# TensorE kept in the order of the program's text, in a kernel of two transformer blocks

## The chip, the core and the metric

The kernel runs on one core of a Trainium2 chip. The core has five engines that run side by side: TensorE (PE in the profile; PEld is its load of weights), VectorE (DVE), ScalarE (ACT), GpSimd (POOL) and SyncE (SP, which here only issues transfers). Each engine takes its instructions strictly from a queue of its own, and semaphores make one engine wait for another. The metric is the device time of one execution, in microseconds, as the median of several runs.

## What is computed

The input is 512 tokens of 1024 features in fp32. Two blocks follow each other. Cut to what matters:

```python
def first_block(x, ...):
    p = split(rms_norm(x, norm_g) @ w_in)                 # q, k, v, o, z, gates, attention parts
    mq, mk = silu(conv4(p.m_q)), silu(conv4(p.m_k))       # causal convolutions over 4 tokens
    mh = mlstm(mq, mk, p.m_v, p.m_i + b_i, p.m_f + b_f)   # 4 heads of 256, running maximum of the gates
    ya = sigmoid(p.m_o) * head_layernorm(mh) * silu(p.m_z)
    kc, vc = gelu(blocks(k) @ w1) @ w2, ...               # compressed keys and values
    yb = sparse_attention(q, kc, vc, ...) * silu(p.n_z)
    x = x + (sigmoid(p.g_a) * (ya @ w_a) + sigmoid(p.g_b) * (yb @ w_b)) @ w_out
    return rms_norm(x, final_g)

def second_block(x, c, ...):
    shift, scale, gate = silu(c) @ ada_w + ada_b
    x = x + 0.5 * gate[0] * swiglu(modulate(rms_norm(x)), ffn1)
    x = x + gate[1] * token_mixer(modulate(rms_norm(x)))  # pooling branch and gated delta rule
    x = x + 0.5 * gate[2] * swiglu(modulate(rms_norm(x)), ffn2)
    return rms_norm(x, final_g)

def gated_delta_rule(q, k, v, g, beta):                   # 8 heads of 128
    a = strict_lower(beta * (k @ k.T) * decay)
    u, w = solve(1 + a, beta * v), solve(1 + a, beta * exp(gc) * k)
    for chunk in chunks:                                  # S: state of 128 x 128
        v_new = u - w @ S
        o = (q * exp(gc)) @ S + (q @ k.T * decay) @ v_new
        S = S * exp(g_last) + k_dec.T @ v_new
```

## The kernel before

Values and weights are split into a high and a low part, both of a type that TensorE multiplies quickly, and each product of fp32 values is three matmuls into the same bank of PSUM: high with high, low with high, high with low. In the rows the parts end in h and l (`hh` and `hl` of the normed h, `uh` and `ul` of the values before the norm's factor, `wh` and `wl` of the weights). ACT rounds a piece of weights or values to the high part, DVE (sometimes POOL) subtracts for the low part. The result of a large product, whatever it is, is called `pg`.

A plan (`block1`, `ffn`, `mixer`) lists the large products group by group; `run` goes through it, piece of weights by piece. After each piece it calls `side_step`, which lets some generators go on by a step each: the side work, that is norms, the mLSTM, the attention, and in the mixer the delta rule. So the text of the program is already an interleaving: 12 matmuls of a large product (four 128-row tiles, three parts each), a few small matmuls of side work, 12 matmuls again.

What the steps of the prediction touch:

- Norms: `sq_add` sums squares on DVE or POOL (`nacc`), ones turn them into column sums (`nsum`), and a broadcast (`rb`) gives every row the factors.
- Gates of the first block (`mlstm_gates`): logarithms of the forget gates (`lf`) go through triangles and ones into a bank `gcol`; a scan on DVE (line 1255) gives the running maximum `mrow`, and four more matmuls put it into the same bank. Score products of the mLSTM are `mS`, from `mqk`, which DVE makes behind the convolutions (`ca`, `ct`).
- Compression: first layer `cps`, second layer `vcp`.
- Delta rule. `delta` prepares a head: transposes `dkt`, `dqt`, `dvt`, decays `dD`, products `dgq`, from which DVE makes `dB` and `ddm`; `dB` goes to memory (`bdr`). `delta_solve` inverts the triangles of 32 tokens of two heads (GS = 2) on DVE: it reads them from memory (`sd`), and 31 columns follow, each a multiply (`svt`) and a subtract (`su`), four columns a step; the result goes to memory twice (`udr`, `tdr`). SOLVE_DELAY = 7 steps later `delta_out` reads it back (`dum`, `dtm`, and `dbm` of `dB`), doubles the blocks on TensorE (`diq`, `diu`, twice), runs the recurrence over four chunks (`dks`, `dy`, `dso` on TensorE, `dws`, `dot` on DVE), applies norm and gate (`dot<-dot,db,zs`), and transposes (`doT`). There are four solves, 0 to 3, for heads 0 and 1, 2 and 3, and so on.

What sets the order: the tile framework has a list scheduler, which puts the instructions of each engine in an order of its own, by its own estimates of when operands are ready. A context, `in_order`, exempts the engines that are named in it:

```python
    def in_order(self, which):
        e = {"P": mybir.EngineType.PE, "A": mybir.EngineType.Activation, "D": mybir.EngineType.DVE,
             "G": mybir.EngineType.Pool}
        return self.tc.manual_schedule(engines={e[w] for w in which})
```

In the kernel before it stands at one place, for ACT and DVE at the beginning of the first block (`block1`, line 732); a few single instructions are kept in their place besides (lines 468, 683). TensorE is scheduled everywhere. By the trace, 540 of 9629 matmuls run later than matmuls that come after them in the text; the last of them ends at about 1494 us.

Of the kernel before, what the change touches and what calls it, by code (L numbers as in the profile page):

```python
# [18 lines left out]
P = 128  # L19
T = 512  # L20
D = 1024
# [7 lines left out]
GS = 2                  # heads whose triangles are solved together  # L29
SOLVE_STEP = 4          # columns of them between two products  # L30
SOLVE_DELAY = 7         # steps until the solved ones are back from memory
NV = 2                  # groups of values, of gates, that start before a norm
# [63 lines left out]
def prep(a):  # L96
    """Lays the inputs out for the loads: name -> array."""
# [4 lines left out]
    w = a["w_in"][0]  # L102
    o = {}
    at = 0
# [53 lines left out]
class Group:  # L158
    """One group of a large product: pieces of weights, and what to do with them."""
# [9 lines left out]
class Call:  # L169
    """A place in the plan where something else is put into the program."""  # L170
# [6 lines left out]
class Builder:  # L177
# [56 lines left out]
    def trr(self, out, in_):  # L234
        """transpose of values that float32r holds"""
        return self.nc.tensor.transpose(out.bitcast(F32R), in_, self.identr)
# [9 lines left out]
    def pow(self, out, in_, n):  # L246
        """out = in ** -0.5"""
        self.nc.gpsimd.tensor_tensor(out, in_, self.mhalf[:, 0:n], OP.pow)
# [34 lines left out]
    def later(self, f, *a):  # L283
        """evacuate now, or when the norm that the values lack is there"""
# [11 lines left out]
    def load(self, upto):  # L296
        """starts the loads of the weights, up to a piece"""
# [8 lines left out]
    def part(self, upto):  # L306
        """splits weights into the two parts that the products take"""
# [15 lines left out]
    def run(self, plan, ahead_dma=3, ahead_split=2):  # L323
# [5 lines left out]
        for g in plan:  # L329
# [6 lines left out]
            for k0, n in g.pieces:  # L336
# [4 lines left out]
                if g.early:  # L341
                    # whole tiles of tokens, one after another: the first in banks of the side work
# [35 lines left out]
                elif g.halves:  # L378
                    if k0 == 0:
                        ps = [self.pg.tile([P, 512], F32, tag="g", name="pg") for _ in range(2)]  # L380
                    if g.mid and k0 + n == g.kts:
                        # the first half of the tokens is done before the second
# [66 lines left out]
    def copies(self):  # L449
        """of the constants, in other types"""  # L450
# [11 lines left out]
    def rows_to_bcast(self, cols4, name, inorder=False):  # L462
        """[128, 4] token columns -> a bank [128, 512] with every row the 512 values"""
# [7 lines left out]
    def colsum(self, sq, ps, c0):  # L471
        """sums over features of sq, as token columns ps[:, c0 + t]"""
# [15 lines left out]
    def rstd(self, ps, c0, name):  # L488
        """token columns: (sum / D + eps) ** -0.5"""
# [6 lines left out]
    def u_add(self, f, x, g, shift=None):  # L496
        """x * g, split, for the products that start before the norm is known; the shift beside it"""
# [8 lines left out]
    def unorm(self, pa, pb):  # L506
        """the product with the norm, and the column that the shift adds"""
# [1455 lines left out]
```

## Time and profile before

| | us |
|---|---|
| three runs | 2001.44, 1997.78, 1995.58 |
| median | 1997.78 |
| span of the profiled execution | 1991.7 |
| TensorE busy in it | 1922.1 |
| VectorE busy | 1142.3 |
| ScalarE busy | 872.8 |
| GpSimd busy | 509.6 |

The profiled execution is one of its own; its span goes from its first to its last instruction. The stages in it: first block to about 707 us, first feed-forward part to 1081, mixer with the delta rule to about 1640, second feed-forward part and final norm to the end.

How to read the rows further down: a group of the timeline gives the start, the duration, the engine, the source line (often that of a helper), the operation, out and inputs, sizes, and in brackets the time that the engine stood idle just ahead, with what ended it. Matmuls overlap: one of 512 columns lasts 0.40 us, and the next starts 0.23 us after it. The granted clock (PEclk) is a share of 2.4 GHz; 0.50 is 1.2 GHz.

### The profile page before, as it was taken

The page shows a single profiled execution, that of the slowest core. Times are in us where ns is not written, and L with a number is a line of the kernel's source. Part 1 is how long each engine was busy: PE and PEld are TensorE (multiplying, and loading weights), DVE is VectorE, ACT ScalarE, POOL GpSimd, SP SyncE. Part 2 cuts the span into 40 slices and gives each one's busy share as a digit, 9 for nine tenths or more (in the row PEclk, how much of TensorE's full clock was granted, in tenths as well). Part 3 has the DMA queues.
Part 4 walks back from the last instruction along what each step waited for, and adds up shares of the span by engine and source line. Part 5 has one row for each costly group of instructions (what it writes and reads, how often), then busy time and mean ns, then how long its engine had stood idle before and what let it go on. Part 6 is the DMA issues. An engine that isn't in the chain of part 4 may idle for free. (4 is left out here: it accounts for less than half of the span.)

```text
span 1991.7 us, 27380 instructions
## 1 busy us (share of the span) xinstructions
PE 1922.1 (97%) x10296; PEld 1586.3 (80%) x10296; DVE 1142.3 (57%) x2059; ACT 872.8 (44%) x1856; POOL 509.6 (26%) x376
## 2 busy tenths in 40 slices
PE   8999999998999999999999999999999999999998
PEld 7779878786677888888888888867778897888887
DVE  7777674746655775333333769768755565333322
ACT  6565654656544443222222555645443343222221
POOL 2454443356621270000001433132210060000000
PEclk9999998999999999999999999999999999999999
DMA  5444445454311423333333233232332333333322
GB/s 182 137 147 143 159 136 174 148 187 160 109 43 37 154 78 102 94 93 92 103 109 109 80 94 88 85 100 67 82 105 85 122 101 96 95 95 95 95 88 72
DMA packets 100118, 216.21 MB, mean 109 GB/s; under 512 B 24721, under 2 KB 35857, under 8 KB 99985
## 3 DMA queue, kind: packets, MB, share of 16 engines
q1 hardware_dynamic: 95232, 208.27, 33.1%
q10 hardware_dynamic: 4752, 6.18, 1.0%
q8 instruction: 81, 1.33, 0.3%
q14 instruction: 53, 0.43, 0.1%
HBM read 206.55 MB, written 7.34 MB: 107 GB/s over the span
## 5 line engine op out<-in xcount | busy, mean ns | idle before, releaser
L217 ACT ACTIVATE wh<-wr 128x1024 fp32r<-128x1024 f32 (+4 forms) x311 | 315.2, 1014 | 643.3 <-issue 366.4
L220 DVE TENSOR_TENSOR wl<-wr,wh 128x1024 fp32r<-128x1024 f32 (+4 forms) x289 | 357.2, 1236 | 390.4 <-ACT wh L217 383.0
L229 PE MATMUL pg<-hh,wh 128*128 128x512 f32 x1240 | 501.2, 404 | 1.3 <-DVE un L220 1.3
L229 PE MATMUL pg<-hl,wh 128*128 128x512 f32 x1240 | 493.0, 398 | 0.9 <-DVE hl L226 0.9
L229 PE MATMUL pg<-hh,wl 128*128 128x512 f32 x1240 | 492.4, 397 | 0.0
L229 PEld LDWEIGHTS pg<-hh,wl 128*128 128x128 f32 x1240 | 234.5, 189 | 54.7 <-issue 0.2
L229 PEld LDWEIGHTS pg<-hh,wh 128*128 128x128 f32 x1240 | 235.4, 190 | 52.4 <-issue 2.1
L229 PEld LDWEIGHTS pg<-hl,wh 128*128 128x128 f32 x1240 | 235.1, 190 | 52.1 <-DVE hl L226 1.4
L220 POOL TENSOR_TENSOR adaw<-adaw,sc 128x512 f32<-128x512 f32 x144 | 216.4, 1523 | 228.5 <-DMA adaw<-in_ada 199.1
L220 POOL TENSOR_TENSOR nacc<-nacc,sq 128x512 f32<-128x512 f32 x34 | 47.6, 1406 | 786.4 <-ACT sq L217 786.3
L229 PE MATMUL pg<-wh,hh 128*128 128x256 f32 (+2 forms) x512 | 161.1, 315 | 11.2 <-ACT ca L217 8.8
L229 PE MATMUL pg<-wh,hl 128*128 128x256 f32 (+2 forms) x512 | 153.2, 302 | 1.0 <-DVE hl L220 0.7
L229 PE MATMUL pg<-wl,hh 128*128 128x256 f32 (+2 forms) x512 | 153.9, 301 | 0.0
L229 PE MATMUL pg<-fah,wh 128*128 128x512 f32 (+1 forms) x374 | 140.1, 382 | 0.0
L229 PE MATMUL pg<-fah,wl 128*128 128x512 f32 (+1 forms) x374 | 139.9, 381 | 0.0
L229 PE MATMUL pg<-fal,wh 128*128 128x512 f32 (+1 forms) x374 | 139.7, 380 | 0.0
L217 ACT ACTIVATE adaw<-adaw 128x512 f32<-128x512 f32 x144 | 90.9, 632 | 111.2 <-POOL adaw L220 109.1
L226 DVE SCALAR_TENSOR_TENSOR ca<-cx,cols,ca 128x511 f32<-128x511 f32 (+2 forms) x120 | 113.8, 948 | 24.3 <-ACT ca L217 22.3
L229 PEld LDWEIGHTS pg<-wh,hh 128*128 128x128 f32 x512 | 98.8, 193 | 21.2 <-ACT ca L217 9.7
L229 PEld LDWEIGHTS pg<-wl,hh 128*128 128x128 f32 x512 | 98.5, 192 | 4.6 <-issue 1.2
L229 PEld LDWEIGHTS pg<-wh,hl 128*128 128x128 f32 x512 | 97.9, 192 | 5.2 <-DVE hl L220 2.1
L220 POOL TENSOR_TENSOR wl<-wr,wh 128x1024 fp32r<-128x1024 f32 (+2 forms) x22 | 48.5, 2206 | 178.3 <-ACT wh L217 160.1
(431 smaller groups left out, 3217.8 us busy)
## 6 DMA issues: line engine op xcount, KB each, us to landing
adaw<-in_ada SPq DMA_DIRECT2D x144, 256.0 KB
wr<-in_f1i SPq DMA_DIRECT2D x44, 512.0 KB
wr<-in_f2i SPq DMA_DIRECT2D x44, 512.0 KB
wr<-in_m_qkv SPq DMA_DIRECT2D x24, 512.0 KB
wr<-in_w_o SPq DMA_DIRECT2D x16, 512.0 KB
wr<-in_f1o SPq DMA_DIRECT2D x16, 512.0 KB
wr<-in_m_g SPq DMA_DIRECT2D x16, 512.0 KB
wr<-in_f2o SPq DMA_DIRECT2D x16, 512.0 KB
```

Of the source, the lines that this page charges most:

```text
L217: return self.nc.scalar.activation(out, in_, f, bias=bias, scale=scale, **k)
L220: return (eng or self.nc.vector).tensor_tensor(out, a, b, op)
L226: return self.nc.vector.scalar_tensor_tensor(out, a, s, b, op0=op0, op1=op1, **k)
L229: return self.nc.tensor.matmul(out, lhsT, rhs, start=start, stop=stop, **k)
```

## The change

`kernel` wraps the whole build in the context, for TensorE alone. DVE, ACT, POOL and SP stay with the scheduler, which orders them anew around the fixed order. Besides, comments and docstrings are gone all over the file; they are left out here.

```diff
@@ -1956,7 +1956,9 @@
     with tile.TileContext(nc) as tc:
         with ExitStack() as ctx:
-            Builder(ctx, tc, A, out, coff).build()
+            b = Builder(ctx, tc, A, out, coff)
+            with b.in_order("P"):
+                b.build()
     r = run_bass_kernel_spmd(nc, [dram], core_ids=[0])
```

What that does to the order shows at three places. (Numbers behind names tell buffers apart; all of those of the changed kernel are higher by two.) First, TensorE at the gates of the first block, before: the columns of `lf`, then products; the columns of `mrow` stand at row 272, behind 27 products.

```order
242 L229 MATMUL pg_663<-hh_454,wl_383 128x512
243 L229 MATMUL gcol_676<-lf_583,cst_91 128x16 x2
244 L229 MATMUL gcol_676<-lf_583,ones_119 128x16
245 L229 MATMUL pg_663<-hh_491,wh_382 128x512
246 L229 MATMUL pg_663<-hl_492,wh_382 128x512
247 L229 MATMUL pg_663<-hh_491,wl_383 128x512
248 L229 MATMUL pg_663<-hh_524,wh_382 128x512
```

The same place on TensorE in the changed kernel:

```order
242 L229 MATMUL pg_665<-hh_456,wl_385 128x512
243 L229 MATMUL gcol_678<-lf_585,cst_93 128x16 x2
244 L229 MATMUL gcol_678<-lf_585,ones_121 128x16
245 L229 MATMUL gcol_678<-cst_93,mrow_652 128x4 x4
246 L229 MATMUL pg_665<-hh_493,wh_384 128x512
247 L229 MATMUL pg_665<-hl_494,wh_384 128x512
248 L229 MATMUL pg_665<-hh_493,wl_385 128x512
```

The columns of `mrow` moved ahead of the 27 products. Second, TensorE at the block inverse of heads 0 and 1 (`diq`), before: the matmuls are strewn among products of a later group, `pg_11664`.

```order
5955 L229 MATMUL pg_11664<-hl_10060,wh_11422 128x512
5956 L229 MATMUL pg_11664<-hh_10059,wl_11423 128x512
5957 L229 MATMUL diq_11516<-dtm_11444,dbm_11445 32x32
5958 L229 MATMUL pg_11664<-hh_10067,wh_11422 128x512
5959 L229 MATMUL pg_11664<-hl_10068,wh_11422 128x512
5960 L229 MATMUL pg_11664<-hh_10067,wl_11423 128x512
5961 L229 MATMUL pg_11664<-hh_10075,wh_11422 128x512
5962 L229 MATMUL pg_11664<-hl_10076,wh_11422 128x512
5963 L229 MATMUL diq_11516<-dtm_11444,dbm_11445 32x32 x7
5964 L229 MATMUL pg_11664<-hh_10075,wl_11423 128x512
```

TensorE at the same matmuls in the changed kernel:

```order
5919 L229 MATMUL pg_11430<-hl_10090,wh_11283 128x512
5920 L229 MATMUL pg_11430<-hh_10089,wl_11284 128x512
5921 L229 MATMUL diq_11518<-dtm_11446,dbm_11447 32x32 x8
5922 L229 MATMUL diq_11530<-dtm_11462,dbm_11463 32x32 x8
5923 L229 MATMUL pg_11556<-hh_9972,wh_11352 128x512
5924 L229 MATMUL pg_11556<-hl_9973,wh_11352 128x512
```

All sixteen moved ahead, in front of the group `pg_11556` (`pg_11554` before) and of `pg_11664`. Third, VectorE at the gates of heads 0 and 1 (`dot<-dot,db,zs`), which TensorE's `doT` waits for, before: columns of solve 1 (`svt`, `su`) stand among them.

```order
1303 L220 TENSOR_TENSOR svt<-sd,su 32x207
1304 L220 TENSOR_TENSOR da<-drq 128x4
1305 L226 SCALAR_TENSOR_TENSOR dot<-dot,db,zs 128x128
1306 L220 TENSOR_TENSOR su<-su,svt 32x23x9
1307 L220 TENSOR_TENSOR da<-da,doss 128x4
1308 L226 SCALAR_TENSOR_TENSOR dot<-dot,db,zs 128x128
1309 L220 TENSOR_TENSOR svt<-sd,su 32x192
1310 L223 TENSOR_SCALAR da<-da 128x4
1311 L226 SCALAR_TENSOR_TENSOR dot<-dot,db,zs 128x128
1312 L220 TENSOR_TENSOR su<-su,svt 32x24x8
1313 L226 SCALAR_TENSOR_TENSOR dot<-dot,db,zs 128x128
1314 L220 TENSOR_TENSOR svt<-sd,su 32x175
```

VectorE at the same gates in the changed kernel:

```order
1315 L226 SCALAR_TENSOR_TENSOR ca<-cx,cols,ca 128x510
1316 L223 TENSOR_SCALAR da<-da 128x4
1317 L226 SCALAR_TENSOR_TENSOR ca<-cx,cols,ca 128x509
1318 L223 TENSOR_SCALAR drq<-drn 128x4
1319 L226 SCALAR_TENSOR_TENSOR db<-db,drq 128x4
1320 L220 TENSOR_TENSOR da<-drq 128x4
1321 L226 SCALAR_TENSOR_TENSOR dot<-dot,db,zs 128x128
1322 L220 TENSOR_TENSOR da<-da,doss 128x4
1323 L226 SCALAR_TENSOR_TENSOR dot<-dot,db,zs 128x128
1324 L226 SCALAR_TENSOR_TENSOR dqkv<-ct,ca 128x512
1325 L223 TENSOR_SCALAR da<-da 128x4
1326 L226 SCALAR_TENSOR_TENSOR dot<-dot,db,zs 128x128 x2
```

The solve moved ahead: its last column stands at row 1307 now, in front of all the gates; before it stood at row 1338, behind them.

## Rows read from the trace of the kernel before

**Rows 1.** The page's first part: busy time, share of the span, instructions of each engine.

```profile
PE 1922.1 (97%) x10296; PEld 1586.3 (80%) x10296; DVE 1142.3 (57%) x2059; ACT 872.8 (44%) x1856; POOL 509.6 (26%) x376
```

**Rows 2.** Table by stage: window, length, then each engine's busy time; last, PEclk, DMA share, GB/s.

```profile
core 0 of [0], span 1991.7 us
...
0.00:90.00 90.00, 76.74 (x465) 66.26 (x466) 68.46 (x114) 58.66 (x114) 27.90 (x24) 0.98 0.47 161
...
1230.00:1495.00 265.00, 251.53 (x1637) 201.30 (x1636) 193.13 (x506) 137.77 (x381) 68.69 (x62) 0.99 0.31 90
1495.00:1979.00 484.00, 482.32 (x2309) 401.06 (x2309) 205.78 (x266) 144.15 (x200) 48.18 (x33) 1.00 0.29 92
```

**Rows 3.** Timeline of PE in the opening: norm sums, gate columns, score products.

```profile
17.45 0.29 PE L229 MATMUL pg<-wl,uh 128*128 128x288 f32 x1
...
22.46 1.05 PE L229 MATMUL nsum<-ones,nacc 128*128 128x1 f32 x8
...
50.67 0.37 PE L229 MATMUL gcol<-lf,ones 128*128 128x16 f32 x2
...
59.87 1.11 PE L229 MATMUL gcol<-cst,mrow 4*128 4x4 f32 x8 [2.47 <-DVE mrow L1255]
...
74.25 1.02 PE L229 MATMUL mS<-mqk 128*128 128x512 f32 x2
...
83.81 2.20 PE L229 MATMUL mS<-mqk 128*128 128x512 f32 x6 [0.55 <-DVE mqk L226]
```

**Rows 4.** Table by stretch, behind one wait and around another; columns as in rows 2.

```profile
60.73:64.15 3.42, 3.42 (x10) 2.73 (x10) 2.17 (x7) 1.34 (x3) 0.92 (x1) 0.50 0.66 236
...
366.00:370.00 4.00, 1.76 (x23) 1.12 (x22) 3.41 (x11) 1.68 (x3) 1.91 (x2) 1.00 0.00 0
```

**Rows 5.** Timeline of PE at the second layer of the compression.

```profile
368.76 0.47 PE L229 MATMUL vcp<-cw,cgl 128*32 128x64 f32 x16 [2.24 <-issue]
```

**Rows 6.** Timeline of DVE at a norm, and of PE at the mixer's first products.

```profile
709.81 1.33 DVE L226 SCALAR_TENSOR_TENSOR ul<-xr,A,uh 128x512 fp32r<-128x512 f32 x1 [1.24 <-ACT uh L217]
...
1103.73 0.70 PE L229 MATMUL pg<-wh,hh 128*128 128x264 f32 x2
...
1105.33 0.64 PE L229 MATMUL pg<-wh,hl 128*128 128x264 f32 x3 [0.30 <-DVE hl L220]
```

**Rows 7.** Timeline of PE in the delta rule: block inverses, transposes, products ahead of their places.

```profile
1232.26 0.39 PE L229 MATMUL pg<-hh,wl 128*128 128x512 f32 x1
1232.49 0.40 PE L229 MATMUL pg<-hh,wh 128*128 128x512 f32 x1
...
1242.84 0.22 PE L229 MATMUL diq<-dtm,dbm 32*32 32x32 f32 x2 [1.82 <-DMA dtm<-tdr]
...
1295.15 0.40 PE L229 MATMUL pg<-hh,wl 128*128 128x512 f32 x1
...
1374.38 0.40 PE L229 MATMUL pg<-hh,wl 128*128 128x512 f32 x1
...
1388.69 0.27 PE L232 MATMUL doT<-cst,dot 128*128 128x128 f32 x1
...
1409.17 0.40 PE L229 MATMUL pg<-hh,wl 128*128 128x512 f32 x1
...
1429.02 0.50 PE L229 MATMUL diq<-dtm,dbm 32*32 32x32 f32 x18
...
1470.08 0.24 PE L229 MATMUL diq<-dtm,dbm 32*32 32x32 f32 x2
```

**Rows 8.** Last gate of heads 0, 1 on DVE; table of two stretches, columns as before.

```profile
1308.28 0.33 DVE L226 SCALAR_TENSOR_TENSOR dot<-dot,db,zs 128x128 f32<-128x128 f32 x1
...
1264.00:1309.00 45.00, 41.42 (x215) 34.03 (x214) 43.42 (x124) 23.45 (x63) 12.48 (x9) 0.96 0.28 90
...
1366.00:1389.00 23.00, 19.86 (x97) 15.78 (x96) 21.52 (x65) 6.48 (x17) 7.72 (x7) 0.93 0.23 81
```

**Rows 9.** Timeline of DVE at the first column of solve 3.

```profile
1425.18 0.18 DVE L220 TENSOR_TENSOR svt<-sd,su 32x31 f32<-32x31 f32 x1 [7.84 <-DMA sd<-bdr]
```

## What I predict, and why

> **What bounds the kernel now.** I read the page's list of engines first: TensorE (PE) is busy 1922.1 of 1991.7 us, VectorE (DVE) 57%, ScalarE (ACT) 44% [rows 1, 2]. So the kernel ends when PE has got through its own work, and all that an order can move is PE's idle time, 69.6 us, and the stretches at half clock. The table by stage comes second [rows 2]. From 1495 us to 1979 us PE is busy 482.32 of 484 us, and there the order by text and the scheduled order agree: nothing lost earlier is given back in that stretch. The other idle lies in the opening (13.3 us in the first 90 us) and in the gated delta rule, 1230 to 1495 us (13.5 us). Third come the single places. PE's order and its text differ there: a small matmul that needs something late is put behind main products that come after it in the text. For each of them I compare two times of the timeline: the end of the product after which the text has it, and its real start. The difference is its **lag**, filled today with work that is ready.
>
> **What the change does.** No instruction is added or taken away. 9629 matmuls keep their durations; a matmul with a lag now stands at its place in the text, and all that follows on PE stands behind it. The price of a place is its lag, less the idle that PE already has there, less whatever the engine that it waits for gains, because PE came late for another reason. I sum five groups of places against the profiled span.
>
> *Opening.* The column sums of the norm have their place at 17.7 us and start at 22.46 [rows 3]: lag 4.7. The broadcast of the gates' running maximum has its place right behind the other gate columns (50.67 + 0.37 = 51.04 us) and starts at 59.87: lag 8.8, of which PE stands idle for 2.47 already, so 6.4 are new. The second pair of score products belongs beside the first, at 74.25 us, and starts at 83.81: lag 9.0 or so. If all three added up, it would be 4.7 + 6.4 + 9, about 20, less some idle just ahead: at most 19. But the scores wait for a DVE chain that goes on during the two earlier waits, and 4.7 + 6.4 already exceeds 9. If DVE also puts the sums ahead of a weight split, the first wait shrinks. I take **+10**, bounds +4 and +19.
>
> *Compression.* Its second-layer matmuls follow a chain behind the first layer and have 2.24 us of idle now [rows 5]. In the text the first-layer matmuls stand 12 products later; at a pitch of 0.23 us, by the first two of [rows 7] that is 2.8 us less cover. **+3**, bounds +1 and +5.
>
> *Norms of the second block.* For the last u part DVE waits 1.24 us and computes 1.33 us [rows 6], while PE runs products that are later in the text: 2.6 us. Two sums and a broadcast behind it move in the same manner. **+5**, bounds +2 and +8.
>
> *First products of the mixer.* The lower halves of h arrive one by one, and PE overtakes with products of the upper half; the first overtaken ones start at 1105.33, 1.6 us behind the products that begin to pass them at 1103.73 [rows 6]. Three such places follow with about 1 us each, and the decay products at the end with about 2; 1.5 of this is idle already. **+5**, bounds +2 and +9.
>
> *Gated delta rule.* Four solves of triangles run on DVE, one for each two heads; memory brings the result back for the matmuls of the block inverse (diq), a recurrence follows, then gates (dot) and transposes (doT).
> - diq of heads 0 and 1: place 1232.65, start 1242.84 [rows 7], lag 10.2, set by DVE and memory. Taken in full.
> - doT of heads 0 and 1: place 1295.55, last gate ready at 1308.61 [rows 8], lag 13.1. DVE is busy 43.42 of 45 us there, so it is not waiting for anyone. The order now puts the whole of solve 1 ahead of these gates; some 4 us of its columns stood between and behind them. That makes 17. If DVE catches up by the 10.2 before, 7 remain. I take 12, the middle, since the wait before also holds products that DVE works from.
> - doT of heads 2 and 3: place 1374.78, the last of them at 1388.69, lag 13.9, of which 12 products (2.8) stand between by the text: 11. DVE is busy 21.52 of 23 us, and 84 rows of solve 2 stand ahead of the gates where 40 did; 44 more, at about 0.3 each, are 13. So 11 to 24, near the lower end because solve 2 then competes less afterwards: 13.
> - diq of heads 4 and 5: place 1409.57, start 1429.02, lag 19.5. Solve 2 is now done earlier by those same rows, and PE is later; between 0 and 19.5 I take 7.
> - diq of heads 6 and 7: start 1470.08, 5.5 behind its place, and their inverse steps stand closer together in the text than they were run: up to 5 more. 6.5.
> - Less the idle that PE has in the stretch: 13.5.
>
> That is 10.2 + 12 + 13 + 7 + 6.5 - 13.5 = **+35**. Bounds: if DVE kept its present times, only the longest lag would count, 19.5 - 13.5 = +6; if each added at its upper end, 10.2 + 17 + 24 + 19.5 + 10.5 - 13.5 = +68.
>
> *Queues.* The scheduled engines get a new order, SP too: the writes and reads of solves 1 and 2 now stand ahead of two weight loads. I cost that at nothing: the DMA share in the delta rule is 0.31 [rows 2], and weights are loaded three pieces ahead. Were that cover gone, a piece of 12 products (2.8 us) would wait.
>
> *Clock.* Behind the wait of 2.47 us PE ran 3.42 us at a granted clock of 0.50, that is at 1.2 GHz [rows 4], which loses 1.7 us; around the wait of 2.24 us it stayed at 1.00. There are ten such losses now, nearly all behind waits of about 2.5 us or more. The new order makes about eight more waits of that length; waits close together share a loss, and a few of the present ones go, so I add **+6** (four times 1.7), bounds 0 and +14.
>
> On the clock the Trainium skill ("TensorE: Matmul & The Clock Gate", "HAM oscillation — how this bites in real kernels") speaks against this change: a stretch of idle sends the array back to half rate, and the loss comes once for each burst. Where every new wait paid for itself the sum would be 8 higher than mine, 2070; the row behind the 2.47 us wait agrees with the rule, the one around 2.24 us shows a wait that cost nothing more.
>
> *Sum:* 10 + 3 + 5 + 5 + 35 + 6 = 64 us. The span of 1991.7 becomes 2055.7; the median of the runs is 6.1 us above the span, and that part doesn't change: 1997.8 + 64, about **2062 us**.
>
> **The rivals.**
> *The other engines adapt (not slower).* The scheduler now plans DVE, ACT, POOL and SP around a fixed PE order, and the text serves the inputs of the later solves sooner: DVE stands idle for 7.84 us before solve 3, waiting for its matrix [rows 9], which the text's products would bring earlier. If every release moved ahead of its place, the waits would vanish with the idle of today: 13.5 us less in the delta rule and no loss elsewhere, 1984 us. It decides from the point where solve 1 and the gates of heads 0 and 1 end 13 us sooner. Against it: DVE is full in just that stretch [rows 8], and the chains of the opening are short dependent steps, which no order shortens.
> *Waits overlap.* DVE keeps its present times, PE's late arrival pays for later lags, and only the longest of each group counts: all groups at their lower bounds, 4 + 1 + 2 + 2 + 6 = 15, and something between this and my sum: 1998 + 15 to 42, centre 2028. For it: much of DVE's delta work depends on earlier DVE work, not on PE. Against it: the products that DVE evacuates stand behind the waits.
> *Everything adds.* All upper bounds: 19 + 5 + 8 + 9 + 68 + 14 = 123, 2121; half of the way from my sum there is 2091. It needs DVE to lose at each place what PE loses.
> *Hardly anything moves.* Only 540 of 9629 matmuls are late against the text, so the kernel might stay at 1998. Against it: late ones are just those that others wait for.
>
> **How the numbers follow.** Mine (2040 to 2080) 0.50; overlap (2013 to 2040) 0.23; adding up (above 2080) 0.15; adapting, 1975 to 2004, 0.08; hardly anything 0.04. The range leaves out the two that are not slower and the far end of the adding: 2014 to 2092. A measurement of this kernel can tell about 0.3%, 6 us. Faster by more takes most of the adapting case, 0.06; within it, with the last case, 0.06; slower 0.88.
>
> **What would show it.** In the profile after: PE's busy share near 94%, idle near 130 us; the list of PE's waits led by doT on dot, diq on the memory transfer, gcol on mrow, with 8 us or more at gcol; the stretch 1495 to the end of before as long as before (497 us). The delta rule should last about 300 us instead of 265. I am wrong if DVE's gates come before PE reaches them, if the opening is not at least 4 us longer, or if PE loses time behind the delta rule.

## The result, and the profile after

| | kernel before | changed kernel |
|---|---|---|
| median of the runs | 1999.5 us (4 runs, 1995.6 to 2001.4) | 2076.4 us (4 runs, 2074.9 to 2079.1) |
| ratio | | 1.0384, 95% interval 1.0366 to 1.0401 |
| span of the profiled execution | 1991.7 us | 2073.1 us |

The change costs 3.84%. The predicted 2062 us was 14 us too low; 2076 lies in the range of 2014 to 2092.

The page's first part, of the changed kernel (busy time, share of the span, instructions of each engine), answers [rows 1]:

```profile
PE 1942.4 (94%) x10296; PEld 1606.3 (77%) x10296; DVE 1143.4 (55%) x2059; ACT 877.6 (42%) x1857; POOL 503.4 (24%) x376
```

The same 10296 instructions on PE: its idle time went from 69.6 to 130.7 us (+61.1), its busy time from 1922.1 to 1942.4 us (+20.3), together the 81.4 us by which the span grew. The busy part goes with the clock: no matmul was added, and the time in which PE was busy at half clock rose from 43.7 to 97.4 us.

The table by stage of the changed kernel (window, length, busy time and count of each engine, then granted clock, share of the DMA engines, GB/s), with stretches moved by PE's delay so that they hold about the work of [rows 2]:

```profile
0.00:110.00 110.00, 83.00 (x487) 72.96 (x488) 70.27 (x117) 63.77 (x127) 35.23 (x27) 0.89 0.41 134
...
1258.00:1576.00 318.00, 265.74 (x1642) 216.38 (x1641) 202.19 (x507) 140.46 (x382) 67.81 (x62) 0.90 0.27 74
1576.00:2060.00 484.00, 482.36 (x2300) 399.68 (x2299) 205.42 (x265) 143.74 (x198) 48.09 (x33) 1.00 0.30 93
```

The delta rule took 318 us instead of 265, its granted clock fell from 0.99 to 0.90, and the last stretch is as full as before: nothing lost ahead of it is given back.

The list of PE's waits of the changed kernel (waiting tile, what released it, total us, times, longest us), its longest ones:

```profile
PE diq L229 <- DMA dtm<-tdr: 15.9, 7, 10.0
PE doT L232 <- DVE dot L226: 12.1, 5, 6.7
PE gcol L229 <- DVE mrow L1255: 9.8, 1, 9.8
PE dso L229 <- ACT dws L217: 8.1, 4, 3.9
PE pg L229 <- ACT uh L217: 7.3, 1, 7.3
...
PE nsum L229 <- DVE nacc L220: 5.6, 1, 5.6
PE mS L229 <- DVE mqk L226: 5.5, 2, 4.2
...
PE pg L229 <- ACT kv L217: 4.1, 3, 1.7
...
PE vcp L229 <- issue: 3.8, 1, 3.8
```

The three at the top are those that the prediction named, and the share of 94%, the idle time near 130 us and the wait of over 8 us at gcol are its signs too. The fourth, dso on dws, it did not have: this is the recurrence.

Both kernels run the same matmuls in nearly the same order, so they can be compared at equal work: the start of the k-th matmul of one less that of the k-th of the other is PE's **delay** at that point. It is worked out here from all matmul rows of the two traces; "of it idle" is what PE's idle time gained in the stage, and the rest is busy time, which grows with half clock:

| place (us in the changed kernel) | delay there | this stage | of it idle | predicted, with bounds |
|---|---|---|---|---|
| end of the opening (250) | 15.0 | +15.0 | +11.9 | +10 (4 to 19) |
| behind the compression (405) | 22.5 | +7.5 | +5.6 | +3 (1 to 5) |
| behind the norms of the second block (750) | 21.5 | -1.0 | +0.7 | +5 (2 to 8) |
| ahead of the mixer (1110) | 20.5 | -1.0 | -0.1 | 0 |
| behind its first products (1150) | 28.1 | +7.6 | +4.0 | +5 (2 to 9) |
| behind the delta rule (1576) | 80.2 | +52.1 | +38.8 | +35 (6 to 68) |
| end | 81.4 | +1.2 | 0.0 | 0; clock +6 (0 to 14) |

The prediction has half clock in a term of its own, so its stages are to be held against the idle column. In the delta rule this can be read from rows: PE was idle for 265 less 251.53 us before [rows 2], and for 318 less 265.74 us now.

### The profile page after: what moved, and what is told of

Its sections match the earlier page's. It is cut to its first block, busy times and chain, and to the rows that moved or that the text cites. A ratio compares the mean times of both kernels' runs of the same rounds, so it can differ in the third digit from the quotient of the medians.

```text
span 2073.1 us, 27408 instructions
## 1 busy us (share of the span) xinstructions
PE 1942.4 (94%) x10296; PEld 1606.3 (77%) x10296; DVE 1143.4 (55%) x2059; ACT 877.6 (42%) x1857; POOL 503.4 (24%) x376
## 5 line engine op out<-in xcount | busy, mean ns | idle before, releaser
L229 PE MATMUL pg<-hh,wh 128*128 128x512 f32 x1240 | 507.0, 409 | 1.6 <-DVE un L220 1.6
L226 DVE SCALAR_TENSOR_TENSOR ca<-cx,cols,ca 128x511 f32<-128x511 f32 (+2 forms) x120 | 119.3, 994 | 13.5 <-ACT ca L217 11.2
```

Source lines behind the costliest of these rows:

```text
L226: return self.nc.vector.scalar_tensor_tensor(out, a, s, b, op0=op0, op1=op1, **k)
L229: return self.nc.tensor.matmul(out, lhsT, rhs, start=start, stop=stop, **k)
```

## The experiments

Times of each kernel are medians of its runs; its ratio is to runs of the kernel before on the same chip.

### Half of the program each

In both, `fix` enters the context for PE and `unfix` leaves it; the edits are to the kernel before, cut to these lines.

```diff
+        plan.append(Call(self.fix))                   (e1)
         plan.append(start(self.delta_gates))
...
         plan.append(Call(self.drain))
+        plan.append(Call(self.unfix))                 (e1)
...
-        self.run(self.block1() + self.ffn(1, 0) + self.mixer() + self.ffn(2, 2))
+        self.run([Call(self.fix)] + self.block1() + [Call(self.unfix)] + self.ffn(1, 0) + ...      (e2)
```

> TensorE keeps the text's order only in the mixer, from the first products on the normed h to the end of the delta rule; the first block is scheduled as before. Theory A (each place pays for the cover that it loses, stage by stage, and nothing is carried over between stages): the delay that the changed kernel gathers in this stretch stays, 20.5 to 80.2 us of it, so about 1999.5 + 60 = 2060 us (2054 to 2066). Theory B (the stages work on each other, for instance because the late first block puts the transfers of the mixer in another position): less than 2050 or more than 2070.

> TensorE keeps the text's order only in the first block; all that follows is scheduled as before. Theory A: the delay that the changed kernel has at the end of the first block stays, 22 to 24 us: 2022 to 2025 us, and this and the run before add up to the whole change. Theory B (the scheduler takes up the delay later by moving work into the waits, since it is free behind the first block): under 2012 us.

Measured: the mixer alone 2053.1 us, ratio 1.0272 (1.0248 to 1.0296); the first block alone 2022.8 us, 1.0128 (1.0100 to 1.0156). The two add up to 4.0%, against 3.84% for the whole change. e2 lies in the band of theory A, e1 is 1 us below it. So within the noise the prices of the two halves are independent: a delay in the first block doesn't pay for a wait in the mixer. That is against the rival in which waits overlap, as far as it is about the two halves.

### A wait moved away from its inputs, and waits filled

e3 sets the steps between the last column of a solve and its matmuls from 7 to 9. e4 puts 146 matmuls whose results are not read into four waits:

```diff
+        self.fill(ps[:, 64:512], 44)                            ahead of gcol <- mrow
+        if h in (0, 4, 5): self.fill(ps, {0: 40, 4: 24, 5: 12}[h])      ahead of diq
+        if h == 2: self.fill(ps, 26)                            ahead of doT
```

> The changed kernel with SOLVE_DELAY 9 in place of 7, so that the block inverse of each pair of heads stands up to 24 products (5.6 us) later in the text and that much more work lies ahead of the matmuls that wait for the solved triangles; the drain at the end may go through a few empty rounds, nothing else. Theory A (lost cover): the wait of 10.0 us at the block inverse of heads 0 and 1 falls to about 4.4, that of 5.9 and 3.1 at heads 4 and 5 to about 3 together, and less half clock behind them; 8 to 15 us less than the changed kernel, 2061 to 2068. Rival (DVE is the bound of the delta rule, PE waits for it in one place or in another): the same time goes to doT and to the steps of the recurrence, less than 3 us gained.

> The changed kernel with matmuls added that nobody reads, just ahead of five waiting matmuls: 44 of 448 columns at the gate columns, 40, 24 and 12 of 512 columns at the block inverses of heads 0, 4 and 5, 26 at the transposes of head 2. They keep TensorE busy in waits that are there anyway. Theory A (of the 81 us about 20 are the half clock behind the waits, which shows as 20.3 us more busy time): the half clock behind these five goes, and the kernel is 6 to 14 us faster than the changed one in spite of 146 matmuls more. Rival (behind the waits the other engines set the pace, so the half clock costs nothing): no change within 3 us, or slower by the added work that sticks out, up to 5.

Measured: e3 2073.1 us, 1.0375 (1.0353 to 1.0396), against 1.0384 for the changed kernel: no gain that can be told. The wait of heads 0 and 1 stayed (10.9 us, the longest of this row):

```profile
PE diq L229 <- DMA dtm<-tdr: 21.0, 9, 10.9
```

With the later place the release came later too, at 1277 us instead of 1271. On the DMA queue the reads that fill dtm and dum moved behind other transfers: the first of dtm was issued at 1273.5 us, in the changed kernel at 1269.0. The write of the result ahead of them (tdr) had come later already, at 1269.1 instead of 1267.0. The scheduler orders the other queues anew for each text, and here a later place brought a later write and a later read. Theory A failed, and of the rival only the number held: the time did not go to doT or the recurrence, it stayed at diq.

e4: 2073.4 us, 1.0380 (1.0353 to 1.0407). Its page's first line and, from its list of waits, the two filled places of the delta rule:

```profile
PE 1970.2 (95%) x10442; PEld 1630.8 (79%) x10442; DVE 1139.7 (55%) x2059; ACT 877.6 (42%) x1857; POOL 501.6 (24%) x376
...
PE doT L232 <- DVE dot L226: 7.7, 10, 2.6
...
PE diq L229 <- DMA dtm<-tdr: 5.3, 9, 1.0
```

The stretches at half clock became shorter by 38 us in all, from 137.3 to 99.5 us. Around the first diq these rows of the two tables show it, of the changed kernel and then of e4:

```profile
1263.00:1281.00 18.00, 8.11 (x93) 6.07 (x94) 6.95 (x19) 4.95 (x9) 1.08 (x2) 0.53 0.35 80
```

```profile
1263.00:1281.00 18.00, 14.64 (x80) 11.22 (x78) 7.95 (x23) 4.90 (x8) 1.09 (x2) 0.82 0.42 96
```

The end came 3 us earlier by the medians, which is not clear of the noise. That is less than the 6 to 14 us of theory A, but it doesn't show that half clock costs nothing. Of the 38 us, 27 were idle time: PE's busy time at half clock fell from 97.4 to 86.8 us only, and at full clock that work would be done 5 us sooner at most. At the first diq the matmuls that were added ran out 1 us ahead of the release, PE then waited three times more for dtm, for 0.4 to 1.0 us each, and the products behind ran at half rate as they had without the filling. One of them in the changed kernel, then in e4 (0.40 us at full clock):

```profile
1275.21 0.63 PE L229 MATMUL pg<-hl,wh 128*128 128x512 f32 x1
```

```profile
1276.41 0.63 PE L229 MATMUL pg<-hl,wh 128*128 128x512 f32 x1
```

At gcol, where the filling reached to 0.6 us of the release, PE stood 3.2 us ahead of the changed kernel at 110 us. Of this 0.7 us were left behind the compression, where PE now waited 5.2 us at vcp instead of 3.8.

### Two DVE steps out, under either order

```diff
-        for j in (1, 2, 3):
+        for j in ((3,) if b is None else (1, 2, 3)):
```

> The changed kernel with two of the three DVE steps of the width-4 convolution left out in the mixer only (taps 1 and 2 of the 24 convolved groups, 0.75 us each: 18 us of DVE work while the mixer's queries, keys and values are made before 1258 us, and 18 us behind it). PE's order and work are unchanged. Theory A (the delay of the delta rule comes from DVE and ACT chains that stand in front of the steps PE waits for; the recurrence waits 3.5 to 4 us because ACT stands at the convolution's tanh, which waits for DVE): the waits of the recurrence (dso on dws) fall below 2 us each, diq of heads 0 and 1 comes 5 to 10 us earlier since solve 0 gets DVE sooner; time 2046 to 2061. Rival B (the waits are set by the places of the solves and by memory, DVE load has no part): time within 8 us of 2076, 2068 to 2078, the longest waits unchanged.

> The control for the kernel with the two convolution steps out: the same two DVE steps left out in the kernel before, whose PE is scheduled. Theory A (there PE fills every wait of the delta rule with products that are ready, so DVE's chains have little to say): 0 to 6 us less than the kernel before, 1990 to 1996. Rival (DVE work sets the delta rule's length in either order): 12 us or more less, below 1984.

Measured: under the order of the text 2055.9 us, 1.0279 (1.0250 to 1.0307), some 20 us less than the changed kernel; under the scheduled order 2-3 us less than the kernel before, 0.9984 (0.9971 to 0.9998). Left out are 48 DVE steps of 0.75 us, 36 us, half of them beside the delta rule. The delay that the delta rule adds fell from 52 to 35 us. The waits of the recurrence, which were 8.1 and 4.0 us, are nearly gone:

```profile
PE dso L229 <- ACT dws L217: 1.8, 4, 0.6
...
PE dy L229 <- ACT dws L217: 1.5, 1, 1.5
```

How DVE comes to stand in front of the recurrence is seen in the timeline of ACT and PE in the changed kernel (start us, us, engine, line, operation, tiles, count, in brackets the idle time before it and what ended it):

```profile
1297.75 0.63 ACT L217 ACTIVATE ct<-ca 128x512 f32<-128x512 f32 x1 [4.20 <-DVE ca L226]
1298.28 0.43 ACT L217 ACTIVATE dws<-dy 128x128 f32<-128x128 f32 x2
```

```profile
1294.40 0.28 PE L229 MATMUL pg<-wh,hl 128*128 128x264 f32 x1
1298.59 0.80 PE L229 MATMUL dso<-dws,dkd 128*128 128x128 f32 x2 [3.91 <-ACT dws L217]
```

ACT's queue has the tanh of a convolution (ct) ahead of the copy that the recurrence needs (dws). The tanh waits 4.20 us for DVE, and the copy behind it waits as long. PE stands 3.91 us behind the copy. The second long wait of dso, 3.52 us at 1382.6 us, has the same tanh ahead of the copy. There DVE's steps on the convolution took 4.90 us, where one takes 0.75 in the median, and POOL was at work beside them without a pause:

```profile
1376.72 4.90 DVE L226 SCALAR_TENSOR_TENSOR ca<-cx,cols,ca 128x511 f32<-128x511 f32 x3 [1.18 <-ACT ca L217]
```

```profile
1375.76 2.41 POOL L220 TENSOR_TENSOR wl<-wr,wh 128x1024 fp32r<-128x1024 f32 x1 [0.41 <-ACT wh L217]
1378.12 1.51 POOL L220 TENSOR_TENSOR dgl<-cst,dgh 128x512 fp32r<-128x512 f32 x1
1379.59 1.49 POOL L220 TENSOR_TENSOR dgl<-cst,dgl 128x512 fp32r<-128x512 f32 x1
```

Theory A held in both orders: with a scheduled PE the same DVE work is hidden. One part of it missed: the first diq came 2.2 us earlier (1268.6 us) instead of 5 to 10, and its wait was still 8.4 us.

### Parts of the delta rule set free again

In e11 the matmuls of the block inverse and the transposes behind the gates, in e12 the recurrence too, may be moved by the scheduler; all else keeps the order of the text.

```diff
-                self.mm(pq[b, c], bv[a, c, b], tv[a, c, 0:32], ...)
+                self.mmf(pq[b, c], bv[a, c, b], tv[a, c, 0:32], ...)     (and the other diq, diu, doT)
-                self.mm(ps[:, 0:P], kT[:, cs(c)], S)
+                self.mmf(ps[:, 0:P], kT[:, cs(c)], S)                    (and dy, dso: e12 alone)
```

> The changed kernel, but the matmuls of the block inverse (diq, diu) and the transposes behind the gates (doT) of the gated delta rule may be moved by the scheduler again; all else on PE, the recurrence (dks, dy, dso) too, keeps the order of the text. Of 540 late matmuls of the kernel before 217 are late again. Theory A (my sum: the price of the delta rule lies at the places of diq and doT): the delay gained from 1230 us on falls from 52 us to 10 us or less, time 2024 to 2036. Rival B (the recurrence has a price of its own, the 23 us that the trace of the changed kernel shows between the places of diq and doT, and it stays): time 2044 to 2056.

> The changed kernel, but the whole output chain of the gated delta rule on PE, block inverse (diq, diu), recurrence (dks, dy, dso) and transposes behind the gates (doT), may be moved by the scheduler again; the main products and the preparation of heads keep the order of the text. 325 matmuls are late against the text (with the inverse and the transposes alone free it were 217, and that gave 2073). Theory A (the chain is one: with the inverse free the recurrence still stood at its place and held the products behind it, so the price comes back; with all of it free the products pass): the delay gained from 1230 us to 1600 us falls from 52 us to 15 us or less, time 2024 to 2040. Rival B (the price lies with the rest that keeps its order, the main products and the preparation of heads): 2055 to 2075, with waits for DVE at pg, dgp or dqt in place of the chain's.

Measured: e11 2073.0 us, 1.0372 (1.0346 to 1.0397); e12 2058.3 us, 1.0297 (1.0280 to 1.0315). From e11's list of waits, then from that of e12:

```profile
PE doT L249 <- DVE dot L243: 13.8, 7, 4.7
...
PE diq L246 <- DMA dtm<-tdr: 7.9, 4, 4.1
...
PE diu L246 <- ACT diq L234: 6.2, 3, 5.1
```

```profile
PE diq L246 <- DMA dtm<-tdr: 12.4, 4, 6.8
PE doT L249 <- DVE dot L243: 11.5, 6, 4.8
```

Neither expectation was right for e11. The first diq cost 5 us of delay instead of 13, but the delta rule as a whole 47 instead of 52. PE's waits in e11 are still led by the matmuls that were free to move: 27.9 us at doT, diq and diu in the rows above, so the order that the scheduler chose has them ahead of their inputs. The recurrences of heads 0 to 3, at their places in the text, cost what they cost in the changed kernel, give or take a us (9.4 and 13.5 us of delay against 8.2 and 13.5).

In e12, with the whole chain free, the delta rule costs 30 us instead of 52. Its time lies in the band of rival B, but the waits that B named (pg, dgp, dqt) did not take the chain's place: 23.9 us of waits are still at diq and doT. So 22 of the 52 us went with the places of the chain. The 30 that are left can't be put down to the matmuls that keep the order of the text, since most of the waits are at free ones. Some 15 of the 30 come where the recurrence of heads 2 and 3 runs. Why the scheduler, with the rest fixed, places free matmuls ahead of their inputs was not separated.

### The opening's wait covered, and POOL's multiplications out

e7 makes the gcol products stand 60 products later in the text. e13b leaves out the 144 multiplications that POOL makes beside the first block for the modulation of the second, e13 is both.

```diff
         yield
+        for _ in range(5):
+            yield
         ps = self.bank("gcol")                                    (e7, e13)
-            self.tt(w, w, sc[i % 2], OP.mult, eng=nc.gpsimd)      (e13b, e13)
```

> The changed kernel with one edit of the text: the small products that broadcast the running maximum of the gates (gcol on mrow) stand some 60 main products later in the text, so that the 9.8 us wait there in the changed kernel has some 16 us of other work ahead of it; the score products (mS) that use them stand 24 products later. Theory A (the price of the opening is the place in the text, and a later place pays it back): the wait at gcol falls below 1 us, the delay against the kernel before at the end of the opening falls from 15 us to 5 to 9 us, and the end comes 6 to 10 us earlier than the changed kernel's 2076: 2066 to 2070. Rival B (the DVE chain behind gcol sets the opening; the wait only moves to the scores or to the weight parts behind them): the delay at the end of the opening stays within 3 us of 15, time 2073 to 2077.

> The changed kernel with the same 144 multiplications of POOL left out and nothing else changed. In the changed kernel the compression's cu step lasted 3.87 us and the compression cost 7.5 us against the kernel before. Theory A (3.6 us of these are the step held up by POOL): the compression costs 3 to 5 us, the end 2068 to 2073, since 7 us of gains in the first block remain at most. Rival B (POOL has no part in it): within 2 us of the changed kernel, 2074 to 2078, the waits of PE at vcp and in front of the compression unchanged.

> The changed kernel with the gcol products 60 products later in the text, and with the 144 multiplications left out that POOL makes beside the first block (1.27 us each; ACT still sums the unmultiplied rows, the number of ACT steps and of loads is unchanged). In that kernel with the multiplications one DVE step of 0.23 us on the compression's path (cu) lasted 8.38 us while POOL ran six steps without a pause, and the delay at the end of the compression rose from 5.5 to 17.3 us. Theory A (DVE was held up by POOL, and this is what gave the opening's gain back): cu takes under 0.5 us, the delay at the end of the compression is 4 to 9 us, the end 2060 to 2067. Rival B (the compression is paced by its own chain of small steps, and the long step is idle time that another step would fill): the delay there stays above 13 us, the end 2070 to 2075.

Measured: e7 2072.9 us, 1.0367 (1.0341 to 1.0392). The wait at gcol is gone and the delay at the end of the opening is 5.5 us instead of 15 to 17; behind the compression it is 17. The end came 3.5 us earlier, which is within the noise: theory A held for the place and not for the time. The gain was given back at the compression, and DVE's timeline shows where, first in the changed kernel and then in e7, and between them POOL's in the changed kernel:

```profile
384.42 3.87 DVE L220 TENSOR_TENSOR cu<-chb 128x66 f32<-128x66 f32 x1 [0.38 <-ACT chb L217]
388.32 0.20 DVE L223 TENSOR_SCALAR cu<-cu 128x66 f32<-128x66 f32 x1
```

```profile
384.42 1.28 POOL L220 TENSOR_TENSOR adaw<-adaw,sc 128x512 f32<-128x512 f32 x1
385.64 0.15 POOL L1788 MEMSET su<- 32x32 f32 x1
385.72 2.48 POOL L220 TENSOR_TENSOR adaw<-adaw,sc 128x512 f32<-128x512 f32 x2
```

```profile
376.50 8.38 DVE L220 TENSOR_TENSOR cu<-chb 128x66 f32<-128x66 f32 x1 [0.45 <-ACT chb L217]
```

A step of 66 columns lasted 3.87 us and 8.38 us, in the kernel before 0.23. It ends 0.1 us behind the last of POOL's steps that ran one behind the other. The Trainium skill ("SBUF — State Buffer", "Who interferes with whom") says that a DVE instruction with two SBUF inputs contends with a GpSimd instruction that reads SBUF. The rows agree: cu, a product of chb with itself, has two inputs. PE waited 3.8 us at vcp behind it, 7.4 us in e7, and the profile puts these down to "issue".

Without POOL's multiplications that step took 0.23 us in e13b and e13, as theory A said. The times came out far below both expectations: e13b 2036.4 us, 1.0184 (1.0163 to 1.0205), e13 2023.9 us, 1.0127 (1.0110 to 1.0144). I had priced the one step on the compression's path, and not the many other DVE steps of the first block that are longer beside POOL (the convolution's 48 steps there take 1.05 us each in the kernel before, 0.75 in e13b). In the table by stage of e13b, from behind the opening to the compression, PE is never idle, at a granted clock of 1.00:

```profile
107.00:304.00 197.00, 197.00 (x1284) 175.88 (x1283) 122.21 (x238) 126.33 (x307) 3.03 (x3) 1.00 0.49 157
```

And the covered gcol is now worth 12.4 us (2036.4 less 2023.9), where it was worth 3.5 with POOL's steps beside it. So most of the opening's price was the place of gcol in the text, as predicted, and it can be bought back with a later place; the chain on DVE and POOL behind it gave the gain back.

### A version faster than both

Is POOL's part one of the order, or of the kernel? The last run keeps the kernel before, PE scheduled, with all of the computation, and lets DVE multiply and sum in one step what POOL multiplied and ACT summed:

```diff
-            self.tt(w, w, sc[i % 2], OP.mult, eng=nc.gpsimd)
             yield
-            self.act(w, w, AF.Copy, accum_out=part[:, i:i + 1])
+            self.stt(w, w, 1.0, sc[i % 2], OP.mult, OP.mult, accum_out=part[:, i:i + 1])
```

> The kernel before, PE scheduled, with the 144 multiplications of POOL (1.30 us each) and the 144 sums of ACT (0.63 + 0.19 us each) replaced by 144 DVE steps that multiply and sum at once (about 0.75 us each, by the three-operand steps of 512 columns: 108 us of DVE time). All of the computation is kept. In the changed kernel without these multiplications the end came 40 us earlier, about 29 of them before 600 us. Theory A (POOL's multiplications hold up DVE under either order, and the kernel before pays for it too: PE is busy 476.9 of the 500 us from 100 to 600 us at a granted clock of 0.97, 23 us idle and some 15 us lost at half clock): even with the new DVE work the end comes 10 to 30 us earlier than the kernel before, 1965 to 1987, PE's waits on ACT's ca and at vcp fall. Rival B (the gain without the multiplications belonged to the fixed order, where each late DVE step stands in front of PE; the scheduled order fills such waits): 1990 to 2000. Rival C (108 us more of DVE work in a stretch where DVE is busy 317 of 500 us cost as much as POOL's steps did): above 2000.

Measured: 1960.5 us, ratio 0.9805 (0.9782 to 0.9827). Its page's first line, and the steps that were added:

```profile
PE 1913.1 (98%) x10296; PEld 1582.1 (81%) x10296; DVE 1157.9 (59%) x2347; ACT 782.2 (40%) x1568; POOL 297.5 (15%) x232
...
L226 DVE SCALAR_TENSOR_TENSOR adaw<-adaw,sc x144: 658/685/1234, 52.3 to 513.5; 128x512 f32<-128x512 f32 x144
L226 DVE DVE_READ_ACCUMULATOR adaw<-adaw,sc x144: 75/83/90, 52.9 to 514.1; 128x1 f32 x144
```

144 times 0.685 + 0.083 us are 111 us of new work for DVE, and yet its busy time grew by 15.6 us only, from 1142.3: by this count some 95 us of what was busy on DVE had been waiting for POOL. In e13b, which adds nothing, DVE's busy time fell by 71 us, from 1143.4 to 1072.2. The one figure is of the scheduled order, the other of the text's. The stretch from 100 to 600 us, in the kernel before and then in this one:

```profile
100.00:600.00 500.00, 476.88 (x2651) 388.82 (x2650) 316.91 (x626) 283.37 (x690) 235.09 (x176) 0.97 0.43 140
```

```profile
100.00:600.00 500.00, 496.27 (x2820) 403.38 (x2818) 345.11 (x915) 213.05 (x472) 51.90 (x52) 0.99 0.43 140
```

PE's idle time there fell from 23.1 to 3.7 us and its lead over the kernel before is 34 us at 500 us, of which 30 are left at the end of the span. Theory A held, and went beyond its band. The kernel also takes 91 us of sums from ACT, whose part was not measured by itself; e13b kept them and gained 40 us.

e14 is also the scheduled partner of e13b, in that neither has POOL's multiplications. PE's delay in e13b against e14 is 15.0 us at the end of the opening, 17.0 behind the compression, 24.1 behind the mixer's first products, 74.0 behind the delta rule and 73.6 at the end. So the fixed order costs nearly as much without POOL's multiplications as with them, 74 instead of 81 us, and the compression then costs 2 us instead of 7.5. (The two kernels differ in the sums too, which ACT makes in e13b and DVE in e14.)

## Why the prediction was right, and where its sizes were wrong

*The rule of the sum*, a place costs its lag less the idle that PE has there, carried the opening, the first products and the first diq. The first diq was released 27.9 us later than before (1242.84 us in [rows 7], now 1270.78), just PE's delay on arriving: an input of the solve that PE makes late makes the solve late.

*Opening*, +10, measured +15, in its bounds. The rows that answer [rows 3]:

```profile
22.10 1.87 PE L229 MATMUL nsum<-ones,nacc 128*128 128x1 f32 x8 [5.63 <-DVE nacc L220]
...
65.32 1.87 PE L229 MATMUL gcol<-cst,mrow 4*128 4x4 f32 x8 [9.82 <-DVE mrow L1255]
...
92.82 2.08 PE L229 MATMUL mS<-mqk 128*128 128x512 f32 x2 [4.21 <-DVE mqk L226]
```

The step that failed here is the discount: I let the DVE chain of the scores run on during the two earlier waits and gave nearly the whole third wait back. It waits 4.21 us all the same. The sums at 22.46 us before come at 22.10 now, so DVE did put them ahead, as the prediction thought possible, for 0.4 us.

*Compression*, +3, measured +7.5, over its bound of 5. The step took the cover of the text as its only price. That price was right: without POOL's multiplications the place costs 2 us (e13b against e14). The chain behind cps was itself longer: 3.6 us of DVE held up by POOL. The trace of before has such steps too (at 364 to 368 us, three of 1.25 to 1.35 us), and the prediction did not look for them.

*Norms of the second block*, +5, measured -1.0, outside its bounds. The step took the lag of the last u part as a wait; but PE's waits on rb, un and ul there sum to 2.0 us, where the kernel before had 3.3: so the products that PE had run ahead seem not to have been needed as cover. *First products*, +5, measured +7.6, in its bounds.

*Delta rule*, +35, measured +52, in its bounds; of this +38.8 is idle time, which is what the +35 stands for. The idle time of PE by places, from tables of the changed kernel between the ends of these places, sums to 52.3 us:

| place | predicted | idle there now |
|---|---|---|
| diq of heads 0, 1 | 10.2 | 12.1 |
| their recurrence | none | 5.9 |
| doT of heads 0, 1 and diq of 2, 3 | 12 | 6.0 |
| recurrence of 2, 3 | none | 5.5 |
| doT of heads 2, 3 | 13 | 9.1 |
| diq of heads 4, 5 | 7 | 9.5 |
| their recurrence | none | 0.4 |
| last two heads | 6.5 | 3.8 |
| idle of before | -13.5 | contained in the rows above |

The set of places was incomplete: I priced the tails of the solves and the gates, and none of the recurrence. The trace of before had it among the late ones. Set against the order of the changed kernel, 180 of the 867 late rows of PE are of dks, dy and dso (a matmul of fp32 leaves two rows). The first dso of the kernel before, for one, has no wait ahead of it, since PE is busy with products that come after it in the text:

```profile
1258.53 0.28 PE L229 MATMUL pg<-wl,hh 128*128 128x264 f32 x1
1258.65 0.38 PE L229 MATMUL dso<-dws,dkd 128*128 128x128 f32 x2
```

In the changed kernel the recurrence holds 11.8 us of idle time. Its two longest waits (3.91 and 3.52 us) stand behind a copy of ACT that is behind the convolution's tanh, and that behind DVE; e8 shows them fall with DVE's work. The doT were priced too high in return: DVE had caught up with the gates while PE waited for the first diq, which the prediction gave as its lower end for heads 0 and 1 and did not take. That the two errors nearly cancel is luck. e11 and e12 show besides that places are no separate terms in a chain: freed matmuls took most of their waits along.

*Clock*, +6, measured +20.3 of busy time, over its bound of 14. This is the term that was mis-sized most, and with it the sum: the five groups gave 58 us of idle time and 61.1 came; the rest of the shortfall, 14 us, is here. Three of the 20 us came in the opening, three at the mixer's first products and 13 in the delta rule. The number of losses was nearly right, nine stretches at half clock more than before where I took eight. The step that failed is the size of one: I priced each at the 3.42 us of [rows 4] and let half of them be shared, but PE's busy time at half clock grew by 54 us, six for each new stretch. (Four times 1.7 is also nearer to 7 than to 6.) And that nearly all of the losses of before stand behind waits of 2.5 us or more was misread: four of the ten stand behind waits of 1.8 to 2.2 us. The rule of the Trainium skill ("TensorE: Matmul & The Clock Gate", "HAM oscillation — how this bites in real kernels"), one loss for each burst of idle, gave an estimate of 2070 us. The rows of the long waits agree with it (0.53 around the first diq), and the measured time lies nearer to this sum than to mine. Whether taking the half clock away would give its time back is open: in e4 too little of it went.

*Rivals.* The other engines did not move their releases ahead of the places (the first diq; e3). Waits did not overlap between the halves (e1 and e2 add up); inside the delta rule they do in part (the first diq and the doT behind it). The time lies halfway between my sum, 2062, and "everything adds", 2091.

## What to carry to other kernels

A fixed order on the engine that is the bound puts the longest chain of the other engines in front of it, and then work that was hidden is paid for: 36 us of DVE steps were worth 2 to 3 us under the scheduled order and 20 us under the text's. Before pricing such an order list every chain that feeds the engine, also those that are on time today, and look in each engine's own queue for what stands ahead of the step that is awaited. And read a long DVE row beside POOL's rows of the same moment: the time that DVE is busy may be time that it waits.

## What was not expected of the hardware

- One DVE step of 0.23 us lasted 8.38 us beside POOL's steps that followed each other without a pause, and it did not get in between them. In the kernel before, at 364 to 368 us, DVE got in behind each of three such steps, with rows of 1.25 to 1.35 us. What makes the difference stays open.
- 144 steps of 1.3 us on POOL went with 71 us of DVE's busy time and 40 us of the end (2076.4 less 2036.4 in e13b), beside a PE that was 94% busy.
- Filling waits with 146 matmuls raised the granted clock there (0.82 instead of 0.53 around the first diq), and yet the products behind the first diq ran at half rate as before (0.63 us each): four short waits of 0.4 to 1.0 us stood between the filling and them.
